# A feed-forward stage that begins with three block products on half of its tokens

## The chip, the core and the metric

The kernel runs on one core of a Trainium2 chip. The metric is the device time of one execution in microseconds (us). PE is TensorE, DVE VectorE, ACT ScalarE, POOL GpSimd, SP SyncE; SBUF and PSUM are the two on-chip memories, and PSUM takes the products.

## The reference

Two layers, each of a feed-forward stage, a mixing stage and a second feed-forward stage, over 512 tokens of width 1024, all in float32. Every matrix product that the change touches is in `_swiglu`, with D_FF = 2816.

```python
def _swiglu(t, w_gate, w_up, w_down):
    return (jax.nn.silu(t @ w_gate) * (t @ w_up)) @ w_down

h = x
for l in range(DEPTH):                                   # DEPTH = 2
    f = _swiglu(_rmsnorm(h, ffn1_pre_g[l]), ffn1_w_gate[l], ffn1_w_up[l], ffn1_w_down[l])
    h = h + 0.5 * _rmsnorm(f, ffn1_post_g[l])
    u = _rmsnorm(h, mix_pre_g[l])
    ...                                                  # three kinds of attention on u, gated and merged
    h = h + _rmsnorm(merged @ w_out[l], mix_post_g[l])
    f = _swiglu(_rmsnorm(h, ffn2_pre_g[l]), ffn2_w_gate[l], ffn2_w_up[l], ffn2_w_down[l])
    h = h + 0.5 * _rmsnorm(f, ffn2_post_g[l])
```

## The kernel before

**Number format.** Every float32 operand is split in two parts that PE can take: a high part, copied by ACT (`split`, L188, or L191 with a scale), and the remainder, a low part, made by DVE (L189, L192). A product is three matmuls, high by high, high by low, low by high (`mm3`, L214 to L216). So each block of weights costs one ACT and one DVE instruction of 128x1024 elements before PE can use it, and each tile of tokens eight PE transposes (L614), two ACT and two DVE instructions of 128x512.

**The stage.** `ffn()` is built four times; the tiles of the four stages are named a0, c0, a1, c1 after their order (first and second feed-forward of layer 0, then of layer 1). The 512 tokens are four tiles of 128, 0 to 3, which come in that order from what runs before: the residual sum and the norm of a tile (`chain`, `normed`, L604, on DVE), then its transposes (`turned`, L614) and the split into `us` (`us_x` in a0, `us_b` in c0 and c1, `us_c` in a1). The waits between these steps are given as PE time (`W_H`, `W_U`, `W_N`), so that a tile's transposes stand among the matmuls of other work.

The 22 column tiles of gate and up are done as follows. Tiles 0 to 19 form five groups of four (`TG`). A group's gate and up are one 2x2 block matrix product, done with seven block products, n = 0 to 6, in place of eight (`gate_up`): n = 0 and n = 1 take the tokens of tiles 0 and 1 as they are, n = 6 those of tiles 2 and 3, and n = 2 to 5 take sums and differences of token halves, which DVE forms (`whole`, `block_sum`, L672, L678) and `parts_of` splits (tiles `ra` and `aga`, `rc` and `agc`). One block product is 24 matmuls of 512 columns into two PSUM banks. Results go to `ca`, `cc` by ACT copies (L742), DVE additions (L744) or ACT's Silu. The weights of n = 2 to 5 are sums of blocks too, formed by DMA that adds (`kta`, `ktc`) or by DVE (L344). The last two column tiles, 20 and 21 (`EARLY`), are a plain pair: 16 row tiles of gate and up, for two column tiles each.

**The order at the start.** The stage's work is a list of jobs in a queue `Q`; a job has weights to load and a generator that emits its matmuls. A scheduler then orders the instructions of each engine, but keeps in program order what is pinned. The first job needs only tiles 0 and 1 (`src.ready((0, 1))`). Before, it is the pair for these two tiles, in matmuls of 256 columns (`halved`, half 0, L826 to L829); then n = 0 of the first group; then half 1 of the pair with tiles 2 and 3 (`src.ready(range(NT))`); then n = 1 and the rest:

```python
        Q.add(ug + uu + start[0], lambda: halved(EARLY, ug, uu, 0), src.ready((0, 1)))
        Q.add([], start[1])
        Q.add([], lambda: halved(EARLY, ug, uu, 1), src.ready(range(NT)))
```

Half 1 also loads ahead up to four blocks in pinned order (`Q.load_ahead`) and starts the sums of token halves (`next(summed)`). In a0, `begin` writes the start out by hand (transposes and splits of tiles 0 and 1 and the splits of `w_ga`, the pair's first gate weights), the vectors and the statistics of the memory input (`vectors`, `mem_stats`, L1086 to L1090) follow the first group, and some constants for the attention (`causal`, `begins`, `sel`, DVE L143 to L158, which wait for selects of POOL, L144 and L150) are made in the same stretch.

Of the kernel before, what the change touches and what calls it, by code (L numbers as in the profile page):

```python
# [9 lines left out]
F32 = mybir.dt.float32  # L10
F32R = mybir.dt.float32r
BF16 = mybir.dt.bfloat16
AF = mybir.ActivationFunctionType
# [9 lines left out]
def kernel(  # L23
# [81 lines left out]
    def stile(shape, tag, name, dt=F32R):  # L105
        return sb.tile(shape, dt, tag=tag, bufs=BUFS[tag], name=name)
# [134 lines left out]
    class Unit:  # L241
# [30 lines left out]
        def loaded(self):  # L272
            self.raw = None
            if self.ring():
                Q.fetched -= 1
            Q.fetch_ahead()
# [11 lines left out]
    class BlockUnit(Unit):  # L288
# [22 lines left out]
        def ring(self):  # L311
            return self.n in self.BLOCKS and self.twin is None

# [6 lines left out]
        def fetch(self):  # L320
            if self.fetched:
                return
            self.fetched = True
            if self.n in self.SUMS:
                i, one, two = self.SUMS[self.n]
                t = self.keep.get(i, self.k0)
                tc.keep_in_program_order(self.block(t, one))
                tc.keep_in_program_order(self.block(t, two, accum_op=ALU.add))
            if self.ring():
                Q.fetched += 1  # L330
                self.raw = stile([P, self.nk, self.ncol], "raw", "raw_" + self.name, F32)
                self.block(self.raw[:], self.BLOCKS[self.n])

        def load(self):
# [13 lines left out]
            if self.raw is not None and not self.lent:  # L348
                self.raw = None
                Q.fetched -= 1  # L350
            Q.fetch_ahead()

# [277 lines left out]
    W_H, W_U = 4.8, (8.0, 7.0, 7.0, 5.7)  # L630
    W_N = (0.0, 0.0, 3.0, 4.0)

# [8 lines left out]
    def ffn(l, src, wg, wu, wd, dst, name, spare, aside=None):  # L641
# [8 lines left out]

        def hidden(f, pg, pu):
            s = tmp(f"s{name}_{f}")
            nc.scalar.activation(s[:], pg[:], AF.Silu)
# [67 lines left out]
        def gate_up(f, n, uns, last_of_top):  # L721
            seeded = ("gb", 1) in st if n == 1 else False
            if n in (0, 1, 2) and not seeded:
                st["gb", SUM[n]] = [pbank("z" if n == 0 and f == TG[0] else "mm", f"pt{name}_{f}_{n}_{e}") for e in range(2)]
            pts = st.pop(("gb", 1)) if n == 1 else st["gb", SUM[n]]
            opens, ends = n in (0, 1, 2), n in (1, 4, 6)
            for un in uns:
                for k in range(un.nk):
                    kk = un.k0 + k
                    for e in range(2):  # L730
                        mm3(pts[e][:], *input_block(n, kk, e), un.h[:, k], un.l[:, k], opens and kk == 0 and not seeded,
                            ends and kk == ND // 2 - 1, free=True)
                        yield 3 * S * PE_US
            i, j = TO[n]
# [18 lines left out]
            if n == 6 and f == TG[-1]:  # L753
                tc.keep_in_program_order(nc.scalar.preload_act_table_set("natural_log_exp_and_others"))

        def feature_major(f, of=(0, 1)):
# [50 lines left out]

        def halved(f, ug, uu, half):
            if half == 0:
                st["p"] = [pbank("mm", f"p{x}{name}_{f + m}") for x in "gu" for m in range(2)]  # L810
            else:
                Q.hold, Q.pinned = False, True
                Q.load_ahead()
                Q.pinned = False
                next(summed)
            c = HALVES[half]

            for uns, pts in ((ug, st["p"][:2]), (uu, st["p"][2:])):
                for low in (False, True):
                    for un in uns:  # L820
                        for k, (m, pt) in itertools.product(range(un.nk), enumerate(pts)):
                            kk, cols = un.k0 + k, slice(m * P, (m + 1) * P)
                            wh, wl = un.h[:, k, cols], un.l[:, k, cols]
                            ah, al = act(kk, c)
                            if low:
                                nc.tensor.matmul(pt[:, c], wh, al, start=False, stop=False, skip_group_check=True)  # L826
                                nc.tensor.matmul(pt[:, c], wl, ah, start=False, stop=kk == ND - 1, skip_group_check=True)
                            else:
                                nc.tensor.matmul(pt[:, c], wh, ah, start=kk == 0, stop=False, skip_group_check=True)  # L829
                            yield (1 + low) * S // 2 * PE_US  # L830
            if half == 1:
                for m in range(2):
                    hidden(f + m, st["p"][m], st["p"][2 + m])

# [106 lines left out]
        ug, uu = (wpair(w[l], ND, EARLY * P, f"{x}{name}_{EARLY}") for x, w in (("g", wg), ("u", wu)))  # L941
        marks["early"] = ug + uu
        for un, place in zip(ug + uu, ("tri", "tri", (spare, spare), (spare, spare))):
            un.tags = place
# [10 lines left out]
        some(1)  # L955
        add_sums()
        some(8)
        if name == "a0":
            Q.add([], vectors)
            Q.add([], lambda: iter(mem_stats() or ()))  # L960
        for g in TG[1:]:
            todo = turns(g)
            some(2)
# [680 lines left out]
    def begin():  # L1644
# [38 lines left out]
        with in_order(nc.scalar, nc.vector):  # L1683
# [88 lines left out]
```

## Time and profile before

| | |
|---|---|
| median of three runs | 2363.33 us (2363.22 to 2365.84) |
| the profiled execution | 2364.29 us, its span 2362.2 us |
| granted PE clock, mean | 0.999 |
| PE busy | 2348.4 us, 11656 matmuls |
| DVE, ACT, POOL busy | 1778.4, 1440.2, 213.0 us |
| from HBM, to HBM | 349.80 MB, 14.68 MB |

Busy times are those of instructions that compute; register, branch and DMA-issuing instructions are not counted. The ends of matmuls are modelled and they overlap, so the step from one start to the next says what one costs. A row of a timeline has the start in us from the span's start, the length, the engine, the line, the operation, output and inputs, the shape, and how many in line the row holds; in brackets stand the idle time before it and what ended that. Names are those of the kernel's tiles without the numbers.

### The profile page before, as it was taken

The page shows a single profiled execution, that of the slowest core. Times are in us where ns is not written, and L with a number is a line of the kernel's source. Part 1 is how long each engine was busy: PE and PEld are TensorE (multiplying, and loading weights), DVE is VectorE, ACT ScalarE, POOL GpSimd, SP SyncE. Part 2 cuts the span into 40 slices and gives each one's busy share as a digit, 9 for nine tenths or more (in the row PEclk, how much of TensorE's full clock was granted, in tenths as well). Part 3 has the DMA queues.
Part 4 walks back from the last instruction along what each step waited for, and adds up shares of the span by engine and source line. Part 5 has one row for each costly group of instructions (what it writes and reads, how often), then busy time and mean ns, then how long its engine had stood idle before and what let it go on. Part 6 is the DMA issues. An engine that isn't in the chain of part 4 may idle for free.

```text
span 2362.2 us, 31098 instructions
## 1 busy us (share of the span) xinstructions
PE 2348.4 (99%) x11656; PEld 1984.4 (84%) x11656; DVE 1778.4 (75%) x2436; ACT 1440.2 (61%) x2329; POOL 213.0 (9%) x242
## 2 busy tenths in 40 slices
PE   9999999999999999999999999999999999999998
PEld 7888888888888898888888888888888888888887
DVE  8766977778776678769787679766787766876696
ACT  6665665577665555566655566656675655555574
POOL 1101100001020001101011110000011100011100
PEclk9999999999999999999999999999999999999999
DMA  8866854222223467759568767632232234686672
GB/s 243 236 173 178 222 187 143 72 72 81 82 71 116 152 196 185 190 159 242 180 179 212 185 187 223 195 102 81 63 90 81 72 127 151 175 228 175 183 218 98
DMA packets 233114, 366.50 MB, mean 155 GB/s; under 512 B 11242, under 2 KB 101634, under 8 KB 232452
## 3 DMA queue, kind: packets, MB, share of 16 engines
q1 hardware_dynamic: 202400, 305.76, 39.5%
q0 software_dynamic: 30560, 58.76, 14.4%
q8 instruction: 91, 1.49, 0.3%
q14 instruction: 59, 0.48, 0.1%
q10 hardware_dynamic: 4, 0.00, 0.0%
HBM read 349.80 MB, written 14.68 MB: 154 GB/s over the span
## 4 chain that ended last, share of the span: by engine, by line
PE 91%; DVE 4%; DMA 2%; ACT 1%; issue 1%; POOL 0%; SPq 0%; DVEq 0%; POOLq 0%; ACTq 0%
PE ptc L216 5%; PE ptc L215 5%; PE ptc L214 5%; PE pta L216 5%; PE pta L214 5%; PE pta L215 5%; PE pg L216 3%; PE pg L214 3%; PE pg L215 3%; PE pdc L216 3%; PE pda L216 3%; PE pdc L214 3%; PE pdc L215 3%; PE pda L215 3%; PE pda L214 3%; PE pb L214 2%
## 5 line engine op out<-in xcount | busy, mean ns | idle before, releaser
L214 PE MATMUL pg<-us_a,wh_wg 128*128 128x512 f32 x384 | 150.9, 393 | 0.0
L216 PE MATMUL pg<-us_a,wl_wg 128*128 128x512 f32 x384 | 149.7, 390 | 0.0
L215 PE MATMUL pg<-us_a,wh_wg 128*128 128x512 f32 x384 | 149.6, 390 | 0.0
L189 DVE TENSOR_TENSOR wl_tc<-ktc,wh_tc 128x1024 fp32r<-128x1024 f32 x80 | 97.4, 1221 | 61.6 <-ACT wh_tc L188 61.5
L189 DVE TENSOR_TENSOR wl_ta<-kta,wh_ta 128x1024 fp32r<-128x1024 f32 x80 | 97.5, 1222 | 56.4 <-ACT wh_ta L188 56.3
L216 PE MATMUL pta<-wh_ta,aga 128*128 128x512 f32 x320 | 124.6, 390 | 0.9 <-DVE aga L189 0.9
L214 PE MATMUL ptc<-wh_tc,agc 128*128 128x512 f32 x320 | 125.2, 391 | 0.0
L214 PE MATMUL pta<-wh_ta,aga 128*128 128x512 f32 x320 | 125.2, 391 | 0.0
L215 PE MATMUL ptc<-wl_tc,agc 128*128 128x512 f32 x320 | 124.5, 389 | 0.0
L215 PE MATMUL pta<-wl_ta,aga 128*128 128x512 f32 x320 | 124.5, 389 | 0.0
L216 PE MATMUL ptc<-wh_tc,agc 128*128 128x512 f32 x320 | 124.5, 390 | 0.0
L188 ACT CAST wh_tc<-ktc 128x1024 fp32r<-128x1024 f32 x80 | 84.0, 1053 | 63.8 <-PE ptc L216 40.8
L188 ACT CAST wh_ta<-kta 128x1024 fp32r<-128x1024 f32 x80 | 84.1, 1053 | 61.3 <-PE pta L216 39.3
L189 DVE TENSOR_TENSOR wl_tc<-raw_tc,wh_tc 128x1024 fp32r<-128x1024 f32 x60 | 73.0, 1222 | 39.6 <-ACT wh_tc L188 39.6
L189 DVE TENSOR_TENSOR wl_ta<-raw_ta,wh_ta 128x1024 fp32r<-128x1024 f32 x60 | 73.1, 1222 | 38.1 <-ACT wh_ta L188 38.1
L215 PE MATMUL ptc<-wl_tc,us_b 128*128 128x512 f32 x240 | 93.6, 390 | 0.0
L214 PE MATMUL ptc<-wh_tc,us_b 128*128 128x512 f32 x240 | 93.5, 391 | 0.0
L216 PE MATMUL ptc<-wh_tc,us_b 128*128 128x512 f32 x240 | 93.1, 389 | 0.0
L188 ACT CAST wh_tc<-raw_tc 128x1024 fp32r<-128x1024 f32 x60 | 62.9, 1052 | 46.8 <-PE ptc L216 40.1
L188 ACT CAST wh_ta<-raw_ta 128x1024 fp32r<-128x1024 f32 x60 | 62.9, 1052 | 43.6 <-PE pta L216 38.3
L216 PE MATMUL pdc<-wh_dc,ac 128*128 128x512 f32 x224 | 87.4, 392 | 0.7 <-DVE ac L189 0.7
L216 PE MATMUL pda<-wh_da,aa 128*128 128x512 f32 x224 | 87.4, 392 | 0.7 <-DVE aa L189 0.7
(533 smaller groups left out, 7414.2 us busy)
## 6 DMA issues: line engine op xcount, KB each, us to landing
raw_wg<-in_w_gate_dram SPq DMA_DIRECT2D x48, 512.0 KB, 3.6
raw_ta<-in_ffn_w_gate_dram SPq DMA_DIRECT2D x44, 512.0 KB, 4.1
raw_tc<-in_ffn_w_gate_dram SPq DMA_DIRECT2D x44, 512.0 KB, 4.6
raw_da<-in_ffn_w_down_dram SPq DMA_DIRECT2D x42, 512.0 KB, 3.8
raw_dc<-in_ffn_w_down_dram SPq DMA_DIRECT2D x42, 512.0 KB, 3.4
kta<-in_ffn_w_up_dram SPq DMA_DIRECT2D x40, 512.0 KB, 6.1
ktc<-in_ffn_w_up_dram SPq DMA_DIRECT2D x40, 512.0 KB, 6.6
raw_wo<-in_w_out_dram SPq DMA_DIRECT2D x24, 512.0 KB, 3.4
```

The source lines that it names most:

```text
L188: both = [nc.scalar.copy(h_ap, src)]
L189: make = lambda: nc.vector.tensor_tensor(l_ap, src, h_ap.bitcast(F32), ALU.subtract)
L214: nc.tensor.matmul(pt, lh, rh, start=start, stop=False, skip_group_check=free)
L215: nc.tensor.matmul(pt, lh, rl, start=False, stop=False, skip_group_check=free)
L216: nc.tensor.matmul(pt, ll, rh, start=False, stop=stop, skip_group_check=free)
```

## The change

The stage now begins with three block products on tiles 0 and 1: n = 0 and n = 1 of the first group and n = 0 of the second (called `ahead`; its result is copied to SBUF by ACT, and copied back into PSUM before n = 2 of that group, which adds to it). The pair follows once all four tiles are there, in matmuls of 512 columns (`plain`, `both`). The weights of `ahead`, of the pair's gate and of its up are loaded and split in place, in pinned order, each as the job before them begins (`in_place`, `after_loading`). The wait of tile 3 (`W_N`) goes from 4.0 to 2.0. In a0, the first product goes through its parts in another order (`by_parts`), `begin` gives the high and low parts in another order, and `vectors` and `mem_stats` move behind the second group.

```diff
-    W_N = (0.0, 0.0, 3.0, 4.0)
+    W_N = (0.0, 0.0, 3.0, 2.0)
...
         def gate_up(f, n, uns, last_of_top):
-            seeded = ("gb", 1) in st if n == 1 else False
+            if f == TG[1] and n == 2:
+                st["c", 0, 0] = st.pop("ahead")
+                st["gb", 0] = seeds("mm", f"pt{name}_{f}_0", [st["c", 0, 0][:, e] for e in range(2)])
+            seeded, ahead = ("gb", 1) in st if n == 1 else False, f == TG[1] and n == 0
...
+            if src.name == "x" and n == 0 and f == TG[0]:
+                yield from by_parts(pts, uns)
+            else:
...
+            if ahead:
+                t = st["ahead"] = stile([P, 2, S], "rs", f"c{name}_{f}_00", F32)
+                for e in range(2):
+                    nc.scalar.copy(t[:, e], pts[e][:])
+                return
...
+        def by_parts(pts, uns):
+            for un in uns:
+                for e in range(2):
+                    for ah, low in ((0, 0), (1, 0), (0, 1)):
+                        for k in range(un.nk):
+                            kk = un.k0 + k
+                            nc.tensor.matmul(pts[e][:], input_block(0, kk, e)[ah], (un.l if low else un.h)[:, k],
+                                             start=kk == 0 and not ah and not low, stop=False, skip_group_check=True)
+                            yield S * PE_US
...
-        def halved(f, ug, uu, half):
...
+        def in_place(units):
+            Q.pinned = True
+            for un in units:
+                un.load()
+            Q.pinned = False
+
+        def after_loading(units, run):
+            def go():
+                in_place(units)
+                yield from run()
+            return go
+
+        def plain(f, ug, uu):
+            in_place(uu)
+            next(summed)
+            pg = [pbank("mm", f"pg{name}_{f + m}") for m in range(2)]
+            yield from both(ug, pg)
+            s = [tmp(f"s{name}_{f + m}") for m in range(2)]
+            for m in range(2):
+                nc.scalar.activation(s[m][:], pg[m][:], AF.Silu)
+            Q.hold, Q.pinned = False, True
+            Q.load_ahead(2)
+            Q.pinned = False
+            next(summed)
+            pu = [pbank("mm", f"pu{name}_{f + m}") for m in range(2)]
+            yield from both(uu, pu)
+            for m in range(2):
+                hidden(f + m, s[m], pu[m])
+
+        def both(uns, pts):
+            for un in uns:
+                for k in range(un.nk):
+                    kk = un.k0 + k
+                    for m, pt in enumerate(pts):
+                        cols = slice(m * P, (m + 1) * P)
+                        mm3(pt[:], un.h[:, k, cols], un.l[:, k, cols], *act(kk), kk == 0, kk == ND - 1, free=True)
+                        yield 3 * S * PE_US
...
-        todo = turns(TG[0])
-        start = next(todo)
-        Q.add(ug + uu + start[0], lambda: halved(EARLY, ug, uu, 0), src.ready((0, 1)))
-        Q.add([], start[1])
-        Q.add([], lambda: halved(EARLY, ug, uu, 1), src.ready(range(NT)))
+        todo, after = turns(TG[0]), turns(TG[1])
+        start, then, ahead = next(todo), next(todo), next(after)
+        marks["early"] = start[0] + then[0]
...
+        Q.add(marks["early"], start[1], src.ready((0, 1)))
+        Q.add([], after_loading(ahead[0], then[1]))
+        Q.add(ahead[0], after_loading(ug, ahead[1]))
+        Q.add(ug + uu, lambda: plain(EARLY, ug, uu), src.ready(range(NT)))
...
-        if name == "a0":
-            Q.add([], vectors)
-            Q.add([], lambda: iter(mem_stats() or ()))
         for g in TG[1:]:
...
+            if name == "a0" and g == TG[1]:
+                Q.add([], vectors)
+                Q.add([], lambda: iter(mem_stats() or ()))
...
-            for hf in range(2):
-                turn(0, hf)
+            turn(0, 0)
             low0 = ug[0].split_from(ug[0].raw[:], later=True)
+            lows[0, 0]()
             for hf in range(2):
                 scaled(1, hf, r)
             turn(1, 0)
-            turn(1, 1)
-            low1 = ug[1].split_from(ug[1].raw[:], later=True)
-            lows[0, 0]()
-            lows[1, 0]()
             low0()
             ug[0].loaded()
+            lows[1, 0]()
+            low1 = ug[1].split_from(ug[1].raw[:], later=True)
+            turn(0, 1)
+            turn(1, 1)
+            low1()
+            ug[1].loaded()
             lows[0, 1]()
             lows[1, 1]()
-            low1()
-            ug[1].loaded()
```

The rest of the diff lets a block's raw weights lie elsewhere than in the ring `raw` (`BlockUnit.ring`, `place`) and gives `hidden` the Silu's result instead of its input.

More of the change, by code (lines that the diff above doesn't have):

```diff
@@ L721, in gate_up @@
         def gate_up(f, n, uns, last_of_top):
-            seeded = ("gb", 1) in st if n == 1 else False
+            if f == TG[1] and n == 2:
+                st["c", 0, 0] = st.pop("ahead")
+                st["gb", 0] = seeds("mm", f"pt{name}_{f}_0", [st["c", 0, 0][:, e] for e in range(2)])
+            seeded, ahead = ("gb", 1) in st if n == 1 else False, f == TG[1] and n == 0
             if n in (0, 1, 2) and not seeded:
-                st["gb", SUM[n]] = [pbank("z" if n == 0 and f == TG[0] else "mm", f"pt{name}_{f}_{n}_{e}") for e in range(2)]
-            pts = st.pop(("gb", 1)) if n == 1 else st["gb", SUM[n]]
-            opens, ends = n in (0, 1, 2), n in (1, 4, 6)
[L727 to L733, printed above, removed]
+                pts = [pbank("z" if n == 0 and f == TG[0] else "mm", f"pt{name}_{f}_{n}_{e}") for e in range(2)]
+                if not ahead:
+                    st["gb", SUM[n]] = pts
+            elif n == 1:
+                pts = st["gb", 1]
+            else:
+                pts = st["gb", SUM[n]]
+            if n == 1:
+                del st["gb", 1]
+            opens, ends = n in (0, 1, 2), n in (1, 4, 6)
+            if src.name == "x" and n == 0 and f == TG[0]:
+                yield from by_parts(pts, uns)
+            else:
+                for un in uns:
+                    for k in range(un.nk):
+                        kk = un.k0 + k
+                        for e in range(2):
+                            mm3(pts[e][:], *input_block(n, kk, e), un.h[:, k], un.l[:, k], opens and kk == 0 and not seeded,
+                                ends and kk == ND // 2 - 1, free=True)
+                            yield 3 * S * PE_US
[4 more added lines that the diff above has]
+                return
             i, j = TO[n]
@@ L806, in park @@
                     nc.sync.dma_start(hsave[t], hT[t][:])
-        def halved(f, ug, uu, half):
[L809 to L833, printed above, removed]
@@ L835, in down_out @@
+        def both(uns, pts):
+            for un in uns:
+                for k in range(un.nk):
+                    kk = un.k0 + k
+                    for m, pt in enumerate(pts):
+                        cols = slice(m * P, (m + 1) * P)
+                        mm3(pt[:], un.h[:, k, cols], un.l[:, k, cols], *act(kk), kk == 0, kk == ND - 1, free=True)
+                        yield 3 * S * PE_US
         def down_out(t, hf, pt, seeded):
```

32 lines of the change are left out of this document (13 added, 19 removed).

## The prediction, made before the changed kernel was run

> **What bounds the kernel now.** I read the page's head and busy times first, then the chain that ended last, then the list of everything TensorE (PE) waited for, then timelines of the stage starts.
>
> ```profile
> span 2362.2 us, 31098 instructions
> PE 2348.4 (99%) x11656; PEld 1984.4 (84%) x11656; DVE 1778.4 (75%) x2436; ACT 1440.2 (61%) x2329; POOL 213.0 (9%) x242
> ...
> PE 91%; DVE 4%; DMA 2%; ACT 1%; issue 1%; POOL 0%; SPq 0%; DVEq 0%; POOLq 0%; ACTq 0%
> ```
>
> PE is busy 2348.4 of 2362.2 us and carries 91% of the chain. So only two things can move the time: the PE time of what it executes, and new or vanished gaps between its instructions. In the list of PE's waits these rows belong to the stage starts that are edited, all in the first stage (a0); below them, from the timelines, the first matmul of that stage and tile 3's normalisation:
>
> ```profile
> PE pta L216 <- DVE aga L189: 0.9, 1, 0.9
> ...
> PE utx L614 <- DVE fx L604: 0.3, 1, 0.3
> PE pga L829 <- ACT w_ga L188: 0.2, 1, 0.2
> ```
>
> ```profile
> 12.56 1.22 PE L829 MATMUL pga<-us_x,w_ga 128*128 128x256 f32 x8 [1.14 <-ACT us_x L191]
> ```
>
> ```profile
> 24.64 1.27 DVE L604 SCALAR_TENSOR_TENSOR fx<-hx,nhx,gqx 128x1024 f32<-128x1024 f32 x1
> ```
>
> The columns of the waits are total, count and longest, in us. No row of that list names the starts of the other three stages (c0, a1, c1), so any PE gap there in the changed kernel is new. The 1.14 us wait of the very first product for the first split tokens stays, whichever product comes first. The other three (0.9 + 0.3 + 0.2 = 1.4 us) belong to the old order and I let them go.
>
> **The products themselves.** Removed per stage: 192 matmuls of 256 columns (the plain pair, two token halves). Added: 96 of 512 columns. The block products are only moved. The price is the step from one start to the next, not the listed duration, since matmuls overlap. PE's timeline, of a1's old pair, of c0's first block product, and of a long plain run:
>
> ```profile
> 1197.00 0.28 PE L827 MATMUL pua<-us_c,wl_ua 128*128 128x256 f32 x1
> ...
> 1198.68 0.28 PE L827 MATMUL pua<-us_c,wl_ua 128*128 128x256 f32 x1
> ...
> 864.20 0.40 PE L216 MATMUL ptc<-wh_tc,us_b 128*128 128x512 f32 x1
> ...
> 867.64 0.39 PE L216 MATMUL ptc<-wh_tc,us_b 128*128 128x512 f32 x1
> 867.87 1.03 PE L614 MATMUL utb<-ident,fb 128*128 128x128 f32 x8
> ...
> 2348.30 0.39 PE L216 MATMUL pdc<-wh_dc,hidc_16l 128*128 128x512 f32 x1
> ...
> 2351.02 0.39 PE L216 MATMUL pdc<-wh_dc,hidc 128*128 128x512 f32 x1
> ```
>
> 256 columns: 1.68 us over 14 steps, 0.120 us. 512 columns: 3.44 over 15 steps (0.229) in the stage start, 2.72 over 12 (0.2267) in the long run; I take 0.2275, between them. Four stages: 768 x 0.120 = 92.2 us become 384 x 0.2275 = 87.4 us, **4.8 us saved** (4.2 to 5.1 by the two ends), 1.2 us a stage. The Trainium skill (TensorE: Matmul & The Clock Gate, "Wait — 56ns, not 53.3ns?") puts a warm step at N/2.4 GHz plus a fixed 2.5 ns, which speaks against most of this: halving the number of matmuls would save only about 1 us (an estimate by its formula), and the sum below would come out 3.8 us higher. The trace has more than that between two halves and a whole (0.240 against 0.2275), in just these matmuls, so the measured steps decide and that outcome gets no chance of its own.
>
> With 1.4 us of old gaps gone, 6.2 us are to be had if no new gap opens.
>
> **What is queued ahead of the new pair.** The order of instructions on each engine of the built program shows the cost. PE now runs n=0 and n=1 of the first group and n=0 of the second ("ahead") on tokens of tiles 0 and 1, three times 24 matmuls, then the pair on all tokens. That hides the splits of tiles 2 and 3 behind 72 x 0.2275 = 16.4 us; before, 96 x 0.120 + 24 x 0.2275 = 17.0 us, the same to 0.6. But before, ACT and DVE had little to do there and waited for PE's transposes. Now four pieces stand in the same short stretch in their queues, and each engine takes its instructions in order: the two adds and one Silu that finish the first group's gate (with its table load), the split of the "ahead" weights, the two splits of the pair's gate weights, then those of its up weights. Their durations (ACT, DVE timelines; x2 rows give two in line):
>
> ```profile
> 53.78 1.06 ACT L746 ACTIVATE ca<-ca 128x1024 f32<-128x1024 f32 x1 [1.90 <-DVE ca L744]
> 1204.42 1.09 ACT L191 ACTIVATE us_c<-utc 128x512 fp32r<-128x512 f32 x2 [3.20 <-PE utc L614]
> 1208.62 1.99 ACT L188 CAST wh_ta<-kta 128x1024 fp32r<-128x1024 f32 x2
> 1210.63 1.28 ACT L653 ACT_TABLE_LOAD   x1
> 52.47 1.28 DVE L744 TENSOR_TENSOR ca<-ca,pta 128x512 f32<-128x512 f32 x2
> 1196.57 1.28 DVE L604 SCALAR_TENSOR_TENSOR fc<-hc,nhc,gqc 128x1024 f32<-128x1024 f32 x1
> 1205.05 1.29 DVE L192 SCALAR_TENSOR_TENSOR us_c<-utc,us_c 128x512 fp32r<-128x512 f32 x2 [3.01 <-ACT us_c L191]
> 1208.53 2.35 DVE L189 TENSOR_TENSOR wl_ta<-raw_ta,wh_ta 128x1024 fp32r<-128x1024 f32 x2
> ```
>
> So: Silu 1.06, a high half of tokens 0.55, a high half of weights 1.0, table load 1.28, an add 0.64, a normalised tile 1.28, a low half of tokens 0.65, a low half of weights 1.17. I follow each stage by these and by PE steps.
>
> *a0.* The first product starts as before within 0.4 us: 12.95, since it now stands behind all 16 transposes. 24 steps of 0.2275 take n=0 to 18.4, and 24 with tile 2's transposes (0.8 to 0.9 for eight, whose row above is 1.03 with the tail) take n=1 to 24.8. "Ahead" then lacks its low weights: they stand on DVE right behind tile 3's normalisation, which ends at 25.9 in the trace and 1.3 earlier in the new queue, where tile 2's two low halves no longer precede it. 24.6 + 1.17 = 25.8 against PE's demand at 25.25, after two matmuls: 0.6 us. "Ahead" ends with tile 3's eight transposes at 31.7. The high half of the pair's first gate weights stands on ACT behind the Silu, and this behind DVE's second add, which stands behind tile 3's low halves (30.4): add to 31.1, Silu to 32.1, cast to 33.15. **Gap 1.45 us.** Four matmuls later PE needs the low half. On DVE that stands behind the constants of the attention stage, which wait twice for POOL:
>
> ```profile
> 30.36 0.77 POOL L144 TENSOR_SCALAR_AFFINE_SELECT c<-c 128x128 f32<-128x128 f32 x1
> 31.16 0.23 DVE L146 CAST causal<-c 128x128 bf16<-128x128 f32 x1 [1.36 <-POOL c L144]
> 31.44 0.48 DVE L149 MEMSET c<- 128x512 f32 x1
> 31.84 1.16 DVE L672 TENSOR_TENSOR ra<-us_x 128x1024 f32<-128x1024 f32 x1
> 32.04 1.43 POOL L150 TENSOR_SCALAR_AFFINE_SELECT c<-c 128x512 f32<-128x512 f32 x1 [0.92 <-PE pta L216]
> 33.51 0.43 DVE L152 CAST begins<-c 128x512 bf16<-128x512 f32 x1 [0.50 <-POOL c L150]
> 35.00 0.68 DVE L157 TENSOR_SCALAR c<-ident 8x8 f32<-8x8 f32 x4
> ```
>
> From the add's end at 31.1: select done 31.5 and its copy 31.75, memset 32.2, one token sum 33.35, second select (1.43 from 32.25) 33.7 and its copy 34.1, second sum 35.2, four small ones 35.8, low half 36.95. PE stands from 34.05 to about 36.9: **gap 2.8 us**. Later needs (the second gate half at 38.1, the up halves at 39.3 and 40.4) come before PE asks. With 0.6 + 1.45 + 2.8 = 4.85 and 0.2 for n=1's low weights, new gaps in a0 are **5.0 us**.
>
> *a1.* The old pair's first half ends at 1198.8 (the 1198.68 row and a step), so it starts 96 x 0.120 = 11.5 earlier, at 1187.3; 48 steps of 0.2275 take n=0 and n=1 to 1198.2. Tile 3's normalisation is the 1196.57 row, ending at 1197.85; now the two "ahead" low halves (2.35) come ahead of it, to 1200.2, and the two adds after it, to 1201.7. Silu to 1202.85, the two gate casts to 1204.8, their low halves to 1206.1; only behind these stand tile 2's token halves, low ones to 1206.8 and 1207.4, although its transposes are long done. Tile 3's transposes reuse the PSUM bank that these read, and in the new PE order they stand behind all 24 "ahead" matmuls, with nothing to cover them: PE is through at 1204.5 (24 steps and tile 2's transposes) and stands until 1206.8 (**2.3**), and the pair then waits for tile 3's high half (behind a cast of the up weights) and low half (behind its low half), ready about 1209.7, another **1.1** net of transposes and two matmuls. 3.4 us.
>
> *c0, c1.* The order is milder: tile 2's token halves precede the gate weights. Counted back in the same way from the 864.20 row (two steps, eight transposes and 11.5 us), c0 starts at 851.35, and n=0 and n=1 end at 862.3. By the same steps, again with two "ahead" low halves and a normalisation in front, the adds end at 864.3, Silu at 867.1, casts at 868.95, low weights at 870.4, tile 3's first low half at 871.05; PE, after two matmuls of the pair, wants it at 869.8. **Gap 1.25 us each**, 2.5 us.
>
> Costed at nothing, with the cover named: eight ACT copies that put "ahead" back into PSUM (0.6 us each, a whole pair before their use, ACT 61% busy); the memory statistics, moved behind the second group, with three table loads more (3 x 1.28 us on ACT, beside a product of 24 x 0.2275 = 5.5 us; without that cover up to 3.8 us). Weight traffic is unchanged, and SP and POOL issue as many transfers as before.
>
> **Sum.** -4.8 - 1.4 + 5.0 + 3.4 + 2.5 = **+4.7 us**. The profiled execution took 2364.29 us by its own time (2.1 beside its span), 0.96 above the median of 2363.33; so 2369.0 against the former and **2368.0** against the median. With handovers that can each be 0.3 us off, a stage may err by 1 us and the sum by 3: 2365 to 2371.
>
> **Rivals.** *The gaps stay closed.* Faster: the casts and low halves are done in ACT's and DVE's idle time and only the 6.2 us count: 2357.1. For it: DVE is idle a quarter of the time, and the token halves of a1 had 3.0 us of idle ahead of them (1205.05 row). Against it: the order puts the waiting Silu in front. It decides for faster only if the new gaps stay under 1.5 us of my 10.9. 0.12.
>
> *Half the gaps.* Table load and weight splits overlap the transposes better than my steps: 5.5 us of gaps, 2362.6, no change. 0.13.
>
> *The moved statistics.* Their table loads sit between PE's last block product of a group and the casts for the next ones; if the cover of 5.5 us is used up, 3.8 us come on top: 2372. 0.14.
>
> *The clock.* Idle PE may lose its clock. The trace's windows (columns: length, then busy us of PE, PEld, DVE, ACT, POOL, then granted clock, DMA share, GB/s):
>
> ```profile
> 2354.00:2358.00 4.00, 1.72 (x15) 1.52 (x13) 3.35 (x9) 1.05 (x5) 0.00 (x0) 1.00 0.34 131
> 2358.00:2363.00 5.00, 0.00 (x0) 0.00 (x0) 0.91 (x3) 0.00 (x0) 0.00 (x0) 0.59 0.29 105
> ```
>
> With 2.3 of 4 us idle the grant is still 1.00, and it falls only in 5 us without any matmul. A gap of 2.8 us is of the first kind; if it were of the second, some 3 to 4 us of half clock would follow, 2 us lost in each of a0 and a1: 2372. 0.07. The Trainium skill (TensorE: Matmul & The Clock Gate, "What's actually happening") has the clock halved after an idle window of about 3.4 us; by that no single gap of mine reaches it, and the time stays with the sum.
>
> That the change does not do what it says is out: the built program has 384 matmuls fewer, four times 96.
>
> **How the numbers follow.** The forecast's case has 0.54. What a measurement of this kernel can tell from no change is about 0.2%, 4.7 us: below 2358.6 is faster, above 2368.1 slower. The forecast's case lies right on the upper edge: half and half, 0.27 each. Slower: 0.27 + 0.14 + 0.07 = 0.48. Same: 0.27 + 0.13 = 0.40. Faster: 0.12. The range from 2359 to 2372.5 leaves out the closed gaps (0.12) and the worst of the two slow rivals (0.06 or so).
>
> **What would show it.** In the new list of PE's waits: the pair's gate product waiting for ACT's cast (1.45) and DVE's low half (2.8) in a0, tile 3's transposes waiting for DVE in a1 (2.3), the pair waiting for token halves in c0 and c1 (1.25 each); and pair steps of 0.2275 us. I am wrong if these rows are missing or sum below 6 us, if PE's busy time falls by much other than 5 us, or if gaps appear far from the stage starts.

## The result, and the profile after

The changed kernel takes 2370.30 us (median of 11 runs, 2368.80 to 2372.53); the kernel before, on the same chip, 2364.87 us (11 runs, 2363.22 to 2365.84). The ratio is 1.0024 (95% interval 1.0015 to 1.0033): slower by 5.4 us. The profiled execution took 2370.30 us, its span is 2367.7.

The head of the changed kernel's page:

```profile
span 2367.7 us, 30334 instructions
PE 2345.5 (99%) x11272; PEld 1964.7 (83%) x11272; DVE 1782.6 (75%) x2436; ACT 1446.5 (61%) x2340; POOL 211.9 (9%) x242
```

PE has 384 matmuls fewer and is busy 2.9 us less, but the span is 5.5 us longer, so PE stands idle 8.4 us more: 22.2 against 13.8. The four largest rows of its list of waits (total, count, longest) have no counterpart before, or a smaller one:

```profile
PE pga L216 <- DVE wl_ga L189: 2.5, 1, 2.5
PE utx L1711 <- DVE fx L1720: 2.2, 1, 2.2
PE pdc L216 <- DVE ac L189: 2.0, 2, 1.6
PE pgc L215 <- DVE us_b L192: 1.7, 2, 0.8
```

To see in which stage the 5.5 us arise, I compare the same matmul in PE's timeline of both kernels: the first down product of a0; of c0; the first down product of the plain pair (`16h`) in c0, a1 and c1. Before:

```profile
238.78 0.48 PE L214 MATMUL pda<-wh_da,aa 128*128 128x512 f32 x1
1074.85 0.48 PE L214 MATMUL pdc<-wh_dc,ac 128*128 128x512 f32 x1
1152.86 0.39 PE L214 MATMUL pdc<-wh_dc,hidc_16h 128*128 128x512 f32 x1
1488.73 0.39 PE L214 MATMUL pda<-wh_da,hida_16h 128*128 128x512 f32 x1
2322.69 0.39 PE L214 MATMUL pdc<-wh_dc,hidc_16h 128*128 128x512 f32 x1
```

After:

```profile
242.88 0.48 PE L214 MATMUL pda<-wh_da,aa 128*128 128x512 f32 x1
1078.37 0.48 PE L214 MATMUL pdc<-wh_dc,ac 128*128 128x512 f32 x1
1158.29 0.39 PE L214 MATMUL pdc<-wh_dc,hidc_16h 128*128 128x512 f32 x1
1494.71 0.39 PE L214 MATMUL pda<-wh_da,hida_16h 128*128 128x512 f32 x1
2328.16 0.39 PE L214 MATMUL pdc<-wh_dc,hidc_16h 128*128 128x512 f32 x1
```

The lag is 4.1 us after a0, 3.5 after c0's gate and up, 5.4 inside c0's down product, 6.0 after a1 and 5.5 after c1. So a0 costs 4.1, the stretch from there to c0's down product, with c0's gate and up in it, saves 0.6 on what a0 left, c0's down product adds 1.9, a1 adds 0.6, c1 saves 0.5. The forecast by stage was +2.4, 0, nothing, +2.2, 0. The total nearly agrees; the parts don't, and the experiments ask why. The lag after a0 is not the same in every execution: PE's first transposes start at 7.62 us in this profile and at 8.53 in the one before, and a second profile of the changed kernel has a lag of 4.7.

**a0's pair.** PE, DVE and ACT of the changed kernel around the pair's start:

```profile
33.84 0.50 PE L214 MATMUL pga<-us_x,wh_ga 128*128 128x512 f32 x1 [1.15 <-ACT wh_ga L188]
...
37.59 0.73 PE L216 MATMUL pga<-us_x,wl_ga 128*128 128x512 f32 x2 [2.55 <-DVE wl_ga L189]
...
39.62 0.63 PE L216 MATMUL pga<-us_x,wl_ga 128*128 128x512 f32 x1
40.05 0.63 PE L214 MATMUL pga<-us_x,wh_ga 128*128 128x512 f32 x1
```

```profile
34.01 0.43 DVE L152 CAST begins<-c 128x512 bf16<-128x512 f32 x1 [0.50 <-POOL c L150]
...
36.31 1.22 DVE L189 TENSOR_TENSOR wl_ga<-raw_ga,wh_ga 128x1024 fp32r<-128x1024 f32 x1
```

```profile
31.80 1.06 ACT L761 ACTIVATE ca<-ca 128x1024 f32<-128x1024 f32 x1
32.77 1.98 ACT L188 CAST wh_ga<-raw_ga 128x1024 fp32r<-128x1024 f32 x2
```

The cast stands behind the Silu and the low half behind the constants, as chained. But the steps after the gap are 0.43 us (39.62 to 40.05), not 0.23. The windows of the changed kernel (length, busy of PE, PEld, DVE, ACT, POOL, granted clock, DMA share, GB/s) show a lower clock behind the gap; cut at the points where the clock changes, it is 0.50 for 3.41 us:

```profile
32.00:36.00 4.00, 1.89 (x8) 0.91 (x6) 3.48 (x8) 4.00 (x6) 2.67 (x3) 1.00 0.47 177
36.00:40.00 4.00, 2.41 (x8) 1.95 (x9) 3.96 (x7) 1.69 (x3) 1.17 (x1) 0.87 0.88 133
...
35.53:38.94 3.41, 1.35 (x6) 1.13 (x7) 3.34 (x9) 2.07 (x3) 1.59 (x2) 1.00 0.68 93
38.94:42.35 3.41, 3.41 (x10) 2.63 (x9) 3.41 (x4) 1.04 (x1) 0.00 (x0) 0.50 1.09 219
```

From 33.84 to the start of n = 2 (60.22, quoted below) PE needs 26.4 us for the pair's 96 matmuls; 96 x 0.2275 + the 2.55 of the gap are 24.4. Of the other 2.0 us the clock is 1.7 (half of 3.41).

### The profile page after: what moved, and what is told of

It reads as the page before. It is cut to its first block, busy times and chain, and to the rows that moved or that the text cites. A ratio compares the mean times of both kernels' runs of the same rounds, so it can differ in the third digit from the quotient of the medians.

```text
span 2367.7 us, 30334 instructions
## 1 busy us (share of the span) xinstructions
PE 2345.5 (99%) x11272; PEld 1964.7 (83%) x11272; DVE 1782.6 (75%) x2436; ACT 1446.5 (61%) x2340; POOL 211.9 (9%) x242
## 3 DMA queue, kind: packets, MB, share of 16 engines
q8 instruction: 88, 1.44, 0.3%
## 4 chain that ended last, share of the span: by engine, by line
PE 91%; DVE 4%; ACT 2%; DMA 2%; issue 1%; POOL 0%; SPq 0%; DVEq 0%; POOLq 0%; ACTq 0%
PE ptc L214 5%; PE ptc L216 5%; PE ptc L215 5%; PE pta L214 5%; PE pta L216 5%; PE pta L215 5%; PE pg L216 3%; PE pg L214 3%; PE pg L215 3%; PE pda L216 3%; PE pdc L216 3%; PE pda L215 3%; PE pda L214 3%; PE pdc L214 3%; PE pdc L215 3%; PE pb L214 2%
## 5 line engine op out<-in xcount | busy, mean ns | idle before, releaser
L189 DVE TENSOR_TENSOR wl_ta<-raw_ta,wh_ta 128x1024 fp32r<-128x1024 f32 x56 | 68.3, 1224 | 41.6 <-ACT wh_ta L188 41.6
L216 PE MATMUL pdc<-wh_dc,ac 128*128 128x512 f32 x224 | 87.3, 391 | 2.0 <-DVE ac L189 2.0
L216 PE MATMUL pda<-wh_da,aa 128*128 128x512 f32 x224 | 87.4, 391 | 0.7 <-DVE aa L189 0.7
L214 PE MATMUL pdc<-wh_dc,ac 128*128 128x512 f32 x224 | 87.7, 391 | 0.4 <-ACT ac L188 0.4
L214 PE MATMUL ptc<-wh_tc,us_b 128*128 128x512 f32 x224 | 87.7, 391 | 0.0
L214 PE MATMUL pda<-wh_da,aa 128*128 128x512 f32 x224 | 87.5, 391 | 0.0
L215 PE MATMUL pda<-wl_da,aa 128*128 128x512 f32 x224 | 87.2, 389 | 0.0
L215 PE MATMUL pdc<-wl_dc,ac 128*128 128x512 f32 x224 | 87.2, 389 | 0.0
```

The source lines that it names most:

```text
L189: make = lambda: nc.vector.tensor_tensor(l_ap, src, h_ap.bitcast(F32), ALU.subtract)
L214: nc.tensor.matmul(pt, lh, rh, start=start, stop=False, skip_group_check=free)
L215: nc.tensor.matmul(pt, lh, rl, start=False, stop=False, skip_group_check=free)
L216: nc.tensor.matmul(pt, ll, rh, start=False, stop=stop, skip_group_check=free)
```

## The experiments

My theory from this trace: the products are cheaper as worked out, and what eats it are short waits on splits, most of it in a0, where a low clock adds to the gap. The rivals were that a0's cost lies in the hand-written start, that the constants in front of the low half are the whole cause of its delay, and that the wide matmuls themselves are not cheaper.

**The constants behind the pair** (all edits are to the changed kernel).

```diff
             Q.weave(begin(), ma["first"])
+            Q.until(ma["first"])
             more_constants()
```

> The constants of the attention stage are made behind the pair instead of ahead of it, nothing else. Theory A (in a0 the low half of the pair's first gate weights stood on DVE behind the constants and their two waits for POOL, and the idle PE then lost its clock): the wait of pga for wl_ga falls from 2.55 us to under 0.5, the granted clock between 36 and 50 us goes from 0.87 and 0.88 back to 1.00, which is 1.7 us more, and the kernel gains about 4 us (2366). Rival B (the clock was lost at the start or by chance and not by this gap): only the 2.2 us of the gap are gained (2368). Rival C (DVE is full there in any case and another wait takes its place): within 1 us of the changed kernel (2370).

Measured: 2370.54 us (8 runs; before 2364.81), ratio 1.0026 (1.0015 to 1.0036). No gain: the wait for `wl_ga` is still 2.4. DVE of this run:

```profile
31.86 3.49 DVE L669 TENSOR_TENSOR ra<-us_x 128x1024 f32<-128x1024 f32 x3
...
36.39 2.35 DVE L189 TENSOR_TENSOR wl_ga<-raw_ga,wh_ga 128x1024 fp32r<-128x1024 f32 x2
```

The scheduler put three token sums and a sum of them where the constants had been, and the low half starts at 36.39 instead of 36.31. So the constants were only what happened to stand there; the cause is the place of the low half in DVE's order.

**The old hand-written start, on top of that** (`begin` in the order of before).

> As e1, and the start written out by hand has the order of before (tile 0 turned whole, then tile 1, low halves later). Theory A (the new order of the start leaves PE idle for 0.7 and 2.2 us around 7 to 10 us, since a low half stands on DVE ahead of tile 1's scaling, and the clock falls to half for some 7 us): PE's start has no wait over 1.5 us, the clock between 7 and 16 us is 1.00 instead of 0.50 to 0.74, n=0 ends about 1.5 us sooner, and of this 0.5 to 1.5 us reach the end beside e1, as ACT and DVE set the pair's start (2365). Rival B (the pause comes from the arrival of the tokens): no difference to e1, clock low all the same. Rival C (the old order delays the first product): 0.5 to 1 us slower than e1.

Measured: 2368.57 us (11 runs), 1.0016 (1.0008 to 1.0025). Rows of this run (n = 1's start, tile 3's transposes, n = 2's start):

```profile
18.17 0.62 PE L214 MATMUL pta<-wh_ta,us_x 128*128 128x512 f32 x2
...
27.95 1.07 PE L613 MATMUL utx<-ident,fx 128*128 128x128 f32 x8 [2.28 <-DVE fx L603]
...
60.16 0.39 PE L214 MATMUL pta<-wh_ta,aga 128*128 128x512 f32 x1
```

And the same two products in the changed kernel:

```profile
19.43 0.62 PE L214 MATMUL pta<-wh_ta,us_x 128*128 128x512 f32 x2
...
60.22 0.39 PE L214 MATMUL pta<-wh_ta,aga 128*128 128x512 f32 x1
```

The new start does cost time: in these two profiles 1.3 us (19.43 against 18.17). It is where the wait for `fx` (2.2) comes from: tile 0's low half now stands on DVE ahead of tile 1's scaling. The two executions don't begin alike, though: PE's first transposes start at 8.52 us here and at 7.62 in the changed kernel's profile. In the six later profiles with the new start whose transposes start at 8.5, n = 1 starts at 20.20 to 21.31, so its price is rather 2.0 to 3.1 us. How much of that the old start wins back is open. In the rows above nothing is left at n = 2, which starts at 60.2 either way, since a wait of tile 3's transposes for DVE takes the place of the old one. But the median is 2.0 us under that of the run with the constants moved alone, while further down, with the token sums pinned as well, the old start gains nothing.

**Shorter waits (`W_N`) for tiles 2 and 3.**

```diff
-    W_N = (0.0, 0.0, 3.0, 2.0)
+    W_N = (0.0, 0.0, 2.0, 1.0)
```

> The waits W_N of tiles 2 and 3 go from 3.0 and 2.0 to 2.0 and 1.0 in c0, a1 and c1, so that the token halves of tile 2 (a1) and half of those of tile 3 (c0, c1) stand on ACT and DVE ahead of the pair's gate weights; nothing else. Theory A (the gaps of 0.83, 0.79 + 0.16 and 0.82 us at these stage starts come from token halves queued behind weights): they fall to 0.2 or less each, and the kernel gains 2 to 2.6 us (2368). Rival B (PE then waits for the normalised tile 3 instead): waits of the transposes for fb and fc of the same size, no change (2370).

Measured: 2367.02 us (11 runs), 1.0008 (0.9999 to 1.0017). c0's and c1's waits for `us_b` are gone from the list and a1's for `us_c` falls from 0.8 to 0.2. The same five matmuls as above show what a stage is worth without those waits:

```profile
244.32 0.48 PE L214 MATMUL pda<-wh_da,aa 128*128 128x512 f32 x1
1079.09 0.48 PE L214 MATMUL pdc<-wh_dc,ac 128*128 128x512 f32 x1
1157.76 0.39 PE L214 MATMUL pdc<-wh_dc,hidc_16h 128*128 128x512 f32 x1
1492.69 0.39 PE L214 MATMUL pda<-wh_da,hida_16h 128*128 128x512 f32 x1
2325.36 0.39 PE L214 MATMUL pdc<-wh_dc,hidc_16h 128*128 128x512 f32 x1
```

Against before, c0's gate and up take 1.3 us less (834.77 from a0's down to c0's, against 836.07), a1 0.9 less (334.93 against 335.87) and c1 1.3 less (832.67 against 833.96). That is the 1.2 us a stage of the cheaper matmuls, kept when nothing new waits. a0 is 5.5 us behind here and is all of the loss. It is 1.4 more than in the changed kernel's profile, with the same code in a0: this execution begins like the one before (transposes at 8.53), so 5.5 is the fairer figure for a0.

**Halves instead of wholes.** The pair keeps its new place but runs in 256 columns again. The pair's values are then not the reference's, so this run serves for its time alone.

```diff
-                        mm3(pt[:], un.h[:, k, cols], un.l[:, k, cols], *act(kk), ...)
+                        for c in HALVES:
+                            mm3(pt[:, c], un.h[:, k, cols], un.l[:, k, cols], *act(kk, c), ...)
```

> The pair of the changed kernel in matmuls of 256 columns again, 192 a stage instead of 96, in the same place and on all tokens; nothing else. Theory A (a matmul of 256 columns steps by 0.120 us, one of 512 by 0.2275): PE's busy time rises by about 5 us and the kernel loses 4.8 us, less what of it fills the gaps at the stage starts (2373.5 to 2375). Rival B (a fixed cost of only 2.5 ns for each matmul): 1 us slower (2371.3).

Measured: 2373.26 us (5 runs), 1.0040 (1.0027 to 1.0054). PE's busy time:

```profile
PE 2349.8 (99%) x11656; PEld 1986.1 (84%) x11656; DVE 1783.0 (75%) x2436; ACT 1446.9 (61%) x2340; POOL 212.2 (9%) x242
```

384 matmuls more cost 4.3 us of PE time; the time itself rises by some 2 to 3 us beside the two measurements of the changed kernel, since slower matmuls cover part of the waits (c0's and c1's fall from 1.7 to 0.9), though the one for `wl_ga` grows to 3.2. The wide matmuls are cheaper, nearly as worked out.

**The changed kernel again.**

> The changed kernel once more. Theory A (the new waits of 1.6 and 0.4 us in c0's down projection are the late arrival of one accumulated block in that execution, with nothing of the change in it): they are smaller or gone in this execution, while the waits of pga, pgc and utc come again within 0.3 us, and the clock in the first 16 us may be whole or half, without a mark on the time. Rival B (the change moves the queue of DMA there): the same 2.0 us again. The time is 2370 either way.

Measured: 2371.22 us (8 runs, 2368.45 to 2372.78), 1.0028 (1.0018 to 1.0038). The waits for `wl_ga`, `fx`, `us_b`, `wh_ga` and `us_c` are there again, within 0.1 us. PE's waits for `ac` in the down products of c0 and c1 are 0.7 together, as in the kernel before, not 2.0: that one changes from one execution to the next. A wait of 0.5 for `ca` (`tha`) is new. In the first profile the wait for `ac` hung on one late block of down weights, which ACT waits for and DVE's `ac` stands behind (1.6 us of the row in its list): ACT's cast of it starts at 1092.60, after 2.24 us of waiting for the block's transfer.

**Pinning the token sums.** With the constants moved, all token sums (`whole`) are kept in program order, behind the pair's weights.

```diff
-            nc.vector.tensor_tensor(t[:], ...)
+            tc.keep_in_program_order(nc.vector.tensor_tensor(t[:], ...))
```

> The constants behind the pair as in e1, and the first sums of token halves held in program order, so that DVE comes to them behind the pair's weights; nothing else. Theory A (what stands on DVE ahead of the low half of the pair's first gate weights makes the second gap in a0; in e1 four token sums took the place of the constants): the wait of pga for wl_ga falls from 2.4 us to 0.5 or less, the granted clock from 36 to 50 us is 1.00, the pair ends about 3.5 us sooner and the kernel gains 3 to 4 us against the changed kernel (2366 to 2367). Rival B (the wait only moves on, to the first product that needs a token sum, or to the low halves of the up weights): a new wait of PE of 1.5 us or more before 70 us, gain under 1.5 us. Rival C (the clock is lost to PE's idle time in the first 12 us): it is lost again between 36 and 50 us or before, gain about 2 us.

> e8 and the shorter waits W_N of e6 together. Theory A (the gaps of a0 and of the other stage starts are independent, and without them the saving of the wider matmuls is left): gain of e8 and of e6 add up, 6 to 7.5 us against the changed kernel, 2363 to 2364, at or a little under the kernel before. Rival B (ACT and DVE are the bound at these starts, each removed gap reappears): 2366 or more.

> e10 and the hand-written start in the order of before. Theory A (in e3 PE's earlier start was given back in a wait for tile 3's normalised tokens, so the start of a0 is set by ACT and DVE): within 0.5 us of e10, with a wait of the transposes for fx of about 2 us, and the clock at 1.00 up to 30 us. Rival B (the start's idle time counts now that the later gaps are gone): 1 to 2 us faster than e10.

Measured: 2374.93 us (5 runs), 1.0044 (1.0032 to 1.0057); with `W_N` = (0, 0, 2, 1) as well 2372.30 (7 runs), 1.0032 (1.0020 to 1.0043); with the old start too 2373.84 (5 runs), 1.0037 (1.0024 to 1.0049). The wait for `wl_ga` is gone and n = 2 can start earlier, 56.1 instead of 60.2, but a longer wait takes its place, of 5.5 to 6.0 us in all three. PE and the windows of the first:

```profile
72.60 0.79 PE L214 MATMUL pta<-wh_ta,aga 128*128 128x512 f32 x1 [5.50 <-ACT aga L188]
```

```profile
36.00:40.00 4.00, 4.00 (x20) 3.28 (x19) 3.49 (x4) 1.57 (x2) 1.13 (x1) 1.00 0.98 202
...
60.00:80.00 20.00, 14.46 (x56) 11.04 (x55) 15.54 (x24) 9.22 (x13) 7.56 (x7) 0.83 0.89 237
```

The last token sum, pinned, now stands on DVE behind work of the next products and behind the constants (it starts at 67.99), so the operand of a later block product comes 5.5 us late, and the clock falls there. What this settles is the clock at the pair: without the gap its grant stays 1.00 at 36 to 40 us.

**Pinning only the first two sums** (the constants moved as well).

```diff
+            if i == 1:
+                tc.keep_in_program_order(ins)
```

> As e8, but only the first two token sums are held behind the pair's weights; the other two are free again, and DVE makes them during the pair. Theory A (the 5.5 us wait of e8 came from the fourth sum, which the pin had moved behind the constants, and not from DVE being full): no wait for aga over 0.9 us, no wait for wl_ga over 0.5 us, the clock from 36 to 80 us is 1.00, and the kernel gains 3 to 4 us against the changed kernel (2366.5 to 2367.5). Rival B (DVE has no room for the sums and the constants behind the pair): a wait of 2 us or more between 55 and 80 us, no gain.

> e12 with the two sums held only in a0, and the shorter waits W_N of e6. Theory A (independent gaps): e12's and e6's gains add up, 2363 to 2364, level with the kernel before. Rival B: 2366 or more.

Measured: 2373.55 us (5 runs, 2369.62 to 2376.61), 1.0041 (1.0028 to 1.0055). The same with `W_N` = (0, 0, 2, 1), and pinned in a0 alone: 2368.28 (11 runs), 1.0016 (1.0007 to 1.0025). In both n = 2 starts at 57.7 and no gap but the 1.05 for `wh_ga` is left at the pair. Both give much of it back some 36 us later, where PE's transposes of `ca` (`tha`) wait 1.9 and 2.4 us for DVE. (Both profiles are the fastest executions of their runs; why the first run's median is 3 us above the changed kernel's, its profile doesn't show.) ACT and DVE of the first of the two ahead of that wait:

```profile
87.72 1.28 ACT L1129 ACT_TABLE_LOAD   x1
...
89.24 1.28 ACT L757 ACT_TABLE_LOAD   x1
...
91.03 1.04 ACT L188 CAST wh_ta<-kta 128x1024 fp32r<-128x1024 f32 x1
```

```profile
92.10 1.23 DVE L189 TENSOR_TENSOR wl_ta<-kta,wh_ta 128x1024 fp32r<-128x1024 f32 x1 [1.60 <-ACT wh_ta L188]
93.24 1.22 DVE L768 SCALAR_TENSOR_TENSOR ca<-ca,ca 128x1024 f32<-128x1024 f32 x1
```

The moved memory statistics (L1129) bring two table loads ahead of the Silu and of a weight cast on ACT; a low half waits on DVE for that cast, and `ca` stands behind the low half. The changed kernel has the same table loads and a wait of none or 0.5 us there; its PE comes 2.5 us later. This chain is read from the trace; no run moves the statistics back.

**The first gate block one product earlier.** This acts on the cause the other way round: `wl_ga` is split before the waiting Silu and adds.

```diff
-        Q.add([], after_loading(ahead[0], then[1]))
-        Q.add(ahead[0], after_loading(ug, ahead[1]))
+        Q.add([], after_loading(ahead[0] + ug[:1], then[1]))
+        Q.add(ahead[0], after_loading(ug[1:], ahead[1]))
```

> e13, and the first of the pair's two gate weights is loaded and split one block product earlier, ahead of tile 2's and tile 3's token halves and of the Silu. Theory A (the last gap in a0, 1.1 us of pga for wh_ga, is the Silu in front of the cast): that wait disappears too, no new one over 0.5 us appears in a0, c0, a1 or c1, and the kernel is 1 us faster than e13 (2362 to 2363), 2 us faster than the kernel before. Rival B (the earlier split delays the token halves, on which the pair also waits): a wait of pga or pgc for us of 1 us or more in two stages, no faster than e13.

> The changed kernel with two edits: the first of the pair's gate weights is loaded and split one block product earlier (as in e14), and the shorter waits W_N (as in e6). Constants and token sums stay where the changed kernel has them. Theory A (in a0 it is only the place of that one weight block in the queues of ACT and DVE that counts, since the constants and sums fit behind it; and e12 and e13 lost part of their gain because the constants, moved, held up POOL's accumulating transfers): no wait of pga over 0.5 us, no new wait over 0.7 us between 55 and 100 us, the clock from 16 to 100 us at 1.00, 2362 to 2364, level with e14 or better and 0 to 2 us faster than the kernel before. Rival B (without the constants moved, the second gate block is late): a wait of pga for wl_ga of 1 us or more, 2365 to 2367.

Measured, on top of the last kernel above: 2364.69 us (11 runs, 2362.98 to 2371.36; before 2364.78), 1.0003 (0.9995 to 1.0012), level with the kernel before, not 2 us faster. With this edit and `W_N` alone: 2365.76 (11 runs, 2363.45 to 2371.49; before 2364.09), 1.0010 (1.0001 to 1.0019). Pair and n = 2 of the first of the two:

```profile
34.23 0.39 PE L214 MATMUL pga<-us_x,wh_ga 128*128 128x512 f32 x1
...
55.99 0.39 PE L214 MATMUL pta<-wh_ta,aga 128*128 128x512 f32 x1
```

96 matmuls in 21.76 us are 0.2267 each: no wait and no low clock in the pair. The wait for `ca` is 0.6 here. Without the pinned sums and with the constants in their old place (the second of the two) the pair still waits 1.1 us, for the second gate block, and the wait for `ca` is 2.0. These two kernels recover most or all of what the change lost, some 4 to 5.5 us; neither is faster than before. In the first of them a0's first down product still starts 2.4 us later than before (241.22 against 238.78). The new start, with its wait for `fx`, is still in it; no run joins this edit to the old start.

## Why the prediction was right or wrong

The time (2368.0 forecast, 2370.3 measured) is in the range and its sign is that of the likeliest outcome: +5.4 us against the kernel before on the same chip, where +4.7 was forecast. The profiled execution took 2370.3 against a forecast of 2369.0. That the sum came so near is luck in part: errors in its terms cancelled.

- *The products, -4.8.* Right. The halves cost 4.3 us more of PE time, the pair's measured step in the undisturbed pair is 0.2267, and three stages keep 0.9 to 1.3 us each once nothing waits.
- *The old gaps of a0, -1.4.* None of the three is in the new list.
- *a0's new gaps, +5.0.* Place and cause are as chained; 1.15 for 1.45 and 2.55 for 2.8. The 0.6 ahead of the second group's product and the 0.2 of n = 1 did not come. Together 3.7.
- *a0's first product "as before within 0.4 us".* This step failed, though its number came out (12.85 for 12.95). The chain took the hand-written order as free; it adds a wait of 2.2 us of tile 1's transposes. This execution began 0.9 us earlier than the one before, which hid it; where the transposes start at 8.5 as before, the first product starts at 14.2. Its 24 matmuls then took 6.6 us and not 5.5 (the granted clock was 0.50 from 10 to 14 us), so n = 1 starts at 19.43 instead of the 18.4 of the working (18.17 with the old order). +1.0.
- *The clock, given 0.07.* It happened in a0 as the rival says, with about the 2 us it names; in a1 it did not, as the gap there stayed short. The step that failed is "a gap of 2.8 us is of the first kind", taken from one row whose window was cut at a round number. In the 3.41 us ahead of the fall (35.53 to 38.94) PE was busy 1.35 and idle 2.06; the run with the old start lost the clock there too, with a single wait of 2.4 us. With these three changes a0 comes to 2.4 - 1.3 + 1.0 + 2.0 = 4.1, as measured, but only for this execution: the 1.0 has its early beginning in it.
- *a1, +3.4.* Mis-sized. The waits are 0.79 and 0.16:

```profile
1210.88 1.25 PE L613 MATMUL utc<-ident,fc 128*128 128x128 f32 x8 [0.79 <-DVE us_c L192]
...
1213.57 0.50 PE L215 MATMUL pga<-us_c,wh_ga 128*128 128x512 f32 x1 [0.16 <-DVE us_c L192]
```

  Tile 3's normalisation ends 11.9 us after the stage's start (DVE, 1203.31 + 1.29, the start at 1192.72); I had 12.9, because I let both low halves push it back whole, though DVE had been idle for part of that time. All behind it comes 1.0 to 1.4 us earlier, and PE fills most of the second wait with the first products of the up weights (`pua`, from 1212.78 on).
- *c0 and c1, +2.5.* Right in place and cause, 0.83 and 0.82 instead of 1.25 each. In c0 ACT's and DVE's chain came as worked out (tile 3's first low half 19.6 us after the stage's start, 19.7 in the working); PE got there 0.4 us later (18.8 for 18.45).
- *Costed at nothing.* The statistics and table loads delay nothing in the first profile of the changed kernel and 0.5 us in the second. When PE gets there earlier the cover runs out, as that rival said: waits for `ca` of 0.6 to 2.4 us in the last four experiments.
- *Not in the sum.* c0's down product lost 1.9 us more in the first profiled execution and nothing in the second. Why the block is late in some executions stays open; I did not test whether the change makes it likelier.

Of what was to be seen in the trace: the pair's two waits and those of c0 and c1 are there, a1's is a third of its size, and PE's busy time fell by 2.9 instead of 5, because slow matmuls, at the start and behind the gap, count as busy too: from a0's n = 2 on, with the one block product that now comes earlier (5.5) taken off, it fell by 3.35, near the 3.6 of the three other stages.

## What to carry to other kernels

Half as many matmuls of twice the width saved about 1.2 us a stage, and a handful of waits of 1 to 2.5 us at the stage starts, with the clock that one of them cost, took more than that back: where PE is 99% busy, look at the order of the splits on ACT and DVE before the matmuls. When a wait is traced to the instruction ahead of it, ask what a scheduler will put in that place: taking the constants away changed nothing, while loading the operand one product earlier brought the wait from 2.5 us to 1.1, and to nothing with two of the sums pinned behind it. Each gap that was closed showed another behind it, so read the list of waits again after every step.

## What the runs showed of the hardware

The clock's grant doesn't go by the length of one gap. Two kernels have a single wait of about 2 us in the same stretch, at the transposes of `ca`; PE and windows of the run with the first gate block earlier and `W_N`:

```profile
92.32 1.09 PE L791 MATMUL tha<-ident,ca 128*128 128x128 f32 x8 [1.98 <-DVE ca L766]
```

```profile
90.25:93.67 3.42, 1.44 (x11) 1.31 (x11) 3.42 (x4) 3.39 (x6) 0.00 (x0) 1.00 0.00 0
93.67:97.08 3.41, 3.41 (x9) 2.64 (x9) 2.71 (x6) 3.41 (x8) 0.00 (x0) 0.50 0.67 167
```

and of the run with the first sums pinned in a0 alone:

```profile
93.89 1.09 PE L793 MATMUL tha<-ident,ca 128*128 128x128 f32 x8 [2.36 <-DVE ca L768]
```

```profile
88.88:92.29 3.41, 2.65 (x16) 2.06 (x14) 1.80 (x2) 3.40 (x5) 0.00 (x0) 1.00 0.12 48
92.29:95.71 3.42, 1.82 (x12) 1.69 (x13) 3.42 (x4) 3.39 (x6) 0.00 (x0) 1.00 0.00 0
95.71:99.12 3.41, 3.41 (x16) 2.81 (x15) 2.23 (x6) 3.41 (x8) 0.00 (x0) 1.00 0.72 180
```

The shorter gap, 1.98 us, cost 3.41 us of half clock, which is 1.7 us of work; the longer one, 2.36, cost nothing.

What decides is where the gap lies. In each of the 14 profiles the clock changes only at points that are a whole number of 3.41 us apart, and between matmuls the half clock lasts one or two such pieces (behind a0's gap in the changed kernel from 38.94 to 42.35). The windows above are cut at these points. The gap of 1.98 us lies whole in one piece, in which PE was busy 1.44 us, and the next piece is at half clock. The gap of 2.36 us is shared by two pieces, busy 2.65 and 1.82, and neither is followed by half clock. From 20 us on, this holds in all 14 profiles: behind every piece at full clock with 1.44 us of busy PE or less the clock is at half, behind every one with 1.54 or more it is not. It is no limit for everything: in the first 10 us, where PE runs only transposes and short preparatory products, pieces with 2.25 to 2.69 us were followed by half clock, and a piece already at half clock stayed there with 2.15. The points lie elsewhere in each execution, so whether a gap of 2 us costs the clock is a matter of chance, and its price should be put in as a chance, not as zero.

The Trainium skill (TensorE: Matmul & The Clock Gate, "What's actually happening") has the clock halved after an idle window of some 3.4 us, and calls that window "free-running". The steps of 0.43 us behind a0's gap agree with the half clock, and the pieces of 3.41 us with the window. But the window need not be idle throughout: a wait of 1.98 us in it was enough.
